# Reordering the last part of an output projection, and the first pair of the MLP behind it, in a decoder layer written as split float32 block products

## The chip, the cores and the metric

The kernel runs on one core of a Trainium2 chip. A core has five engines that run their own instruction streams side by side: TensorE (PE in the profile; its weight loads are PEld), VectorE (DVE), ScalarE (ACT), GpSimd (POOL) and SyncE (SP, which here only issues DMAs). Each stream runs in its written order, and semaphores tie the streams together. Matmul results land in PSUM; everything else lives in SBUF.

The metric is the device time of one launch in microseconds (us), the median of several runs. Lower is better.

## The reference

One decoder layer on x of shape 1 x 1024 positions x 1024 channels, all float32:

```python
h = rmsnorm(x, mix_norm[l])
proj = h @ w_in[l]
q, k, v, su, sv, g_a, g_b = jnp.split(proj, splits, axis=-1)
y_att = sliding_window_attention(q, k, v, q_norm[l], k_norm[l], sinks[l])
y_sgu = chunked_spatial_gating(su, sv, sgu_norm[l], w_s[l], b_s[l])
merged = (jax.nn.sigmoid(g_a) * (y_att @ w_oa[l])
          + jax.nn.sigmoid(g_b) * (y_sgu @ w_ob[l]))
x = x + merged @ w_out[l]
x = x + conv_gated_mlp(rmsnorm(x, ffn_norm[l]), w_up[l], conv_w[l], conv_b[l], w_down[l])
```

The change sits at `merged @ w_out` (the output projection, 1024 x 1024 x 1024), the squares for the second rmsnorm, and the first pair of column blocks of `@ w_up` (1024 x 5632).

## The kernel before

**Split float32.** A float32 operand is written as a high part (a float32r copy, made by ACT in `copy_hi`, L88) and a low part (the operand minus its high part, made by DVE for the moving side, by POOL for the weights). A product is three matmuls: high x high, high x low, low x high. So each operand costs one ACT copy and one subtraction before TensorE can use it.

**Seven products.** Large products are cut into 2 x 2 blocks and computed with seven block products in place of eight. The left side (weights) gives A11, A12, A22 and the sums S1 to S4; the right side (activations) gives B11, B21, B22 and the sums T1 to T4. The pairs are A11 B11, A12 B21, S1 T1, S2 T2, S3 T3, S4 B22 and A22 T4. Some products accumulate in PSUM onto a copy of another's result.

**The output projection** is 14 jobs, `out_job(0)` to `out_job(13)`. Job j works on product j // 2 of `O_STEPS` and on half e = j % 2 of the output rows: jobs 4 and 5 are S2 T2, 6 and 7 S1 T1, 8 and 9 S4 B22, 10 and 11 S3 T3, 12 and 13 A22 T4. A job is 24 matmuls (L1629) onto one of four PSUM tiles of 128 x 1024, X[0], X[1], Y[0], Y[1]. X[e] and Y[e] are reused: after jobs 4 and 5 an ACT copy (L1587) puts X[e] into Y[e], and S1 T1 accumulates on it.

`run_jobs` writes out the order. For job j it issues the matmuls, then the extra work that `O_WORK[j]` holds, then the split of the weights of job j + 2 (`o_split`: one ACT copy into `wjh`, two POOL subtractions into `wjl`, L1560), the load of the weights of job j + 4, and then the work on the result of job j, `o_post`. The `wjh` and `wjl` tiles are two deep, so the split for job j + 2 waits until TensorE has finished job j.

`o_post` forms a quarter of the new x (`final`, DVE, L1525), copies it out of PSUM (`keep`, ACT, L1520, and two stores), and makes the right-hand operands of the next product: `right_split`, `right_hi` and `right_lo` write the high and low parts of B11, T1, B22, T3, B21 (L88, L1503, L1510), `stt` (L1539) makes the sums B and Y. `square` takes a kept quarter to the square (ACT, L1531) and adds it to a running sum (POOL, L1533 and L1536). `o_late` holds a split that is run in the next job's `o_post`.

`m_hi`, `m_lo` (L1422) and `m_sum` (L664, L668) make the right-hand operands of the projection itself from `merged`.

**The first pair.** The MLP's up projection takes two column blocks (a pair) at a time: seven products of 12 matmuls each (L1112) onto `zg` (halves g0, g1) and `zv` (halves v0, v1). Each pair's left operands come from `Left`: `load_p`, `load_q`, `load_s3` load the raw blocks, `adds` makes S3 and S1 by two accumulating DMAs from POOL's queue (L1029, L1030), `sums_r` makes S2 and S4 on POOL (L664), and `split_p` (A11, A12), `split_q` (S1, A22), `split_s3` and `split_r` split them: ACT for the high part (L88), POOL for the low part (L1071). For pair 0 (`w0`) these are called from inside the projection. `first_pair` then issues pair 0; its `zv` and `zg` are the PSUM tiles that held Y[0] and Y[1]. Between its products stand the sum of squares over the channels (`ssq_cols`, 16 small matmuls, L1656), the power that makes the scale (POOL, L131), and, after the first product of pair 1, `rms_rows` (16 small matmuls, L140), which spreads the scale over the rows. From pair 1 on `fast_pair` repeats to pair 21.

Of the kernel before, what the change touches and what calls it, by code (L numbers as in the profile page):

```python
# [40 lines left out]
def body(ctx, tc, nc, a):  # L41
# [8 lines left out]
    def nm(s):  # L50
        uid[0] += 1
        return f"{s}_{uid[0]}"
# [1363 lines left out]
    def m_split(n, g):  # L1416
        m_hi(n, g)
        m_lo(n, g)
# [108 lines left out]
    def square(n, e):  # L1527

        q = pools["sq2"][:, (L, H)[int(n[1]) - 1]]
        t = pools["fp"].tile([128, 2, 512], F, tag="sqt", name=nm("sqt"))  # L1530
        nc.scalar.activation(t, ob[n][:, 2 * e:2 * e + 2, :], AF.Square)  # L1531
        if n in ("11", "12") and e == 0:
            nc.gpsimd.tensor_tensor(q, t[:, 0, :], t[:, 1, :], op=ALU.add)  # L1533
        else:
            for k in (0, 1):
                nc.gpsimd.tensor_tensor(q, q, t[:, k, :], op=ALU.add)  # L1536
# [18 lines left out]
    def o_split(r):  # L1555
# [8 lines left out]
        0: lambda: (m_hi("B21", 0), m_hi("B22", 0), out_load("11"), out_load("21")),  # L1564
        1: lambda: (m_split("T2", 0), m_split("T2", 1), m_lo("B22", 0), out_load("22")),
        2: lambda: (m_split("B22", 1), out_load("12")),
        3: lambda: (m_sum("T4", 0), m_sum("T4", 1), m_sum("T3", 0), m_sum("T3", 1)),
        4: lambda: (m_split("T4", 0), square("11", 0), w0.load_p(), w0.load_s3(), w0.load_q()),
        5: lambda: (m_split("T4", 1), square("11", 1), w0.adds()),
        6: lambda: (b11(0), m_split("T3", 0)),  # L1570
        7: lambda: (b11(1), m_split("T3", 1), w0.sums_r()),
        12: lambda: w0.split_s3(),
    }

    def b11(e):
        right_split("B11", e, ob["B"][:, 2 * e:2 * e + 2, :])

    def o_post(s, e):

        X, Yb = ob["X"][e], ob["Y"][e]  # L1580
        A, B = ob["A"], ob["B"]
        ds = (2 * e, 2 * e + 1)
        n = (None, "11", "21", "22", "12", "22", "21")[s]
        gs = [gain(n, d) for d in ds]
        ac = ob[n][:, 2 * e:2 * e + 2, :]
        if s == 2:
            nc.scalar.copy(Yb, X)  # L1587
        final(n, e, X if s in (2, 5, 6) else Yb, ac if s in (2, 3) else X if s == 6 else Yb,
              1.0 if s in (1, 4) else -1.0)
        for f in o_late:  # L1590
            f()
        o_late.clear()
        if s in (1, 4):
            for i, d in enumerate(ds):
                nc.scalar.activation((B if s == 1 else A)[:, d, :], Yb[:, i, :], AF.Copy, scale=gs[i][0])
            keep(n, e, Yb)
        if s in (5, 6):
            m, p = ("B22", Yb) if s == 5 else ("B21", X)
            for i, d in enumerate(ds):
                right_hi(m, d, p[:, i, :], gs[i][0])  # L1600
            keep(n, e, p)
            for i, d in enumerate(ds):
                right_lo(m, d, p[:, i, :], gs[i][0])
# [4 lines left out]
        if s == 5:  # L1608
            for i, d in enumerate(ds):
                stt(B[:, d, :], Yb[:, i, :], gs[i][1], B[:, d, :], ALU.subtract)  # L1610
            for i, d in enumerate(ds):
                stt(Yb[:, i, :], Yb[:, i, :], gs[i][1], A[:, d, :], ALU.add)
            o_late.append(lambda: right_split("T3", e, Yb))

    o_late = []
    SQ_AFTER = {9: ("12", 0), 10: ("12", 1), 12: ("22", 0), 13: ("22", 1)}

    def out_job(j):
        s, e = divmod(j, 2)
# [2 lines left out]
        def main(w):  # L1622
# [10 lines left out]
            yield  # L1633
            if j == 0:
                ob["Y"] = [PS("pY").rearrange("p (d c) -> p d c", d=2) for _ in range(2)]
            if s == 6:
                (w0.split_p, w0.split_q)[e]()
            if s == 0:
                nc.scalar.copy(ob["Y"][e], ob["X"][e])
            else:  # L1640
                o_post(s, e)
            if j in SQ_AFTER:
                square(*SQ_AFTER[j])
            if j == 13:
                psum["P"] = [psA, psA, psC_[0], psC_[0]]

# [89 lines left out]
    def first_pair():  # L1736
# [8 lines left out]
        fx = pools["fp"].tile([128, 4, 512], R, tag="hA", name="fax")  # L1745

        q.prod(q.v1, "A11", "B11")
        nc.scalar.copy(x1, q.v1)
        w.split(("S2", "S4"), w.r, *(fx[:, 2 * i:2 * i + 2, :].rearrange("p a (b m) -> p (a b) m", m=128)
                                     for i in (0, 1)))  # L1750
        nx.load_p()
        q.prod(q.g1, "S1", "T1")
        for e in (0, 1):
            right_split("T2", e, ob["B"][:, 2 * e:2 * e + 2, :])
        nc.scalar.copy(u2, q.g1)
        nx.load_q()
        nx.load_s3()
# [16 lines left out]
        nc.vector.tensor_tensor(q.g0, q.g0, x1, op=ALU.add)  # L1774
# [396 lines left out]
```

## Time and profile before

| | us |
|---|---|
| median of 3 runs (lowest to highest) | 1189.49 (1188.97 to 1190.51) |
| the profiled execution | 1190.27 |
| its span, first to last instruction | 1188.5 |
| TensorE busy in the span | 1164.3 (98%) |
| VectorE, GpSimd, ScalarE busy | 864.5, 664.4, 588.3 |
| mean granted TensorE clock | 0.993 |

The page gives the busy time of each engine, the span in 40 slices, the chain of work that ended last and the costliest groups. A busy TensorE there is not TensorE at its peak: matmuls are pipelined, and a matmul record of 0.39 us stands every 0.23 us. So the questions go to the timelines (each row: start, length, engine, line, operation, output <- inputs, and in brackets the idle time before it and what ended it) and to the table of waits (engine and tile that waited, who was waited for, total us, times, longest).

### The profile page before, as it was taken

How to read it: one execution, taken by the hardware profiler on the slowest of the kernel's cores; microseconds unless marked ns; L12 is line 12 of the kernel's file. 1: busy time of each engine (PE TensorE's matmuls, PEld its weight loads, DVE VectorE, ACT ScalarE, POOL GpSimd, SP SyncE). 2: the span in 40 equal slices, each digit the busy share in tenths (PEclk: the TensorE clock that was granted, in tenths of full speed). 3: DMA queues.
4: the chain of work that ended last, by engine and by line, in shares of the span. 5: the costliest groups of instructions: out<-in, count | busy, mean ns of one | idle time of the engine just before them, and what ended most of it. 6: DMA issues, size and time to landing. Idle time of an engine off the chain costs nothing.

```text
span 1188.5 us, 15815 instructions
## 1 busy us (share of the span) xinstructions
PE 1164.3 (98%) x5784; PEld 983.3 (83%) x5784; DVE 864.5 (73%) x985; ACT 588.3 (50%) x894; POOL 664.4 (56%) x460
## 2 busy tenths in 40 slices
PE   9999999999999999897999999999999999999998
PEld 9899999888888778685878888888888888888886
DVE  6787747635447889876788788877888797876674
ACT  6665668643436545565444444444344445425231
POOL 0668675589775756766967677776867641000000
PEclk9999999999999999998999999999999999999999
DMA  9343565275638665633645455455545258975561
GB/s 368 134 143 66 137 209 193 72 234 156 195 103 274 216 205 206 175 124 107 155 129 168 120 146 155 138 144 134 168 129 168 77 200 286 358 239 195 172 226 53
DMA packets 86429, 204.37 MB, mean 172 GB/s; under 512 B 9616, under 2 KB 17296, under 8 KB 86160
## 3 DMA queue, kind: packets, MB, share of 16 engines
q1 hardware_dynamic: 77280, 174.93, 42.7%
q0 software_dynamic: 8544, 19.93, 10.1%
q10 hardware_dynamic: 528, 8.52, 2.1%
q8 instruction: 45, 0.74, 0.2%
q14 instruction: 32, 0.26, 0.1%
HBM read 162.70 MB, written 57.41 MB: 185 GB/s over the span
## 4 chain that ended last, share of the span: by engine, by line
PE 79%; DVE 10%; POOL 4%; ACT 3%; issue 2%; DMA 2%; SPq 0%; DVEq 0%; POOLq 0%; ACTq 0%
PE pz L1112 46%; PE pdx L1983 8%; PE pd L1983 7%; PE pu L94 1%; PE pu L92 1%; PE pu L93 1%; PE pvs L92 1%; PE pvs L94 1%; PE pvs L93 1%; PE pv L560 1%; PE pq L92 1%; PE pq L94 1%; PE pq L93 1%; PE pY L1629 1%; DMA ra<-wdown 1%
## 5 line engine op out<-in xcount | busy, mean ns | idle before, releaser
L1112 PE MATMUL pz<-T,qh 128*128 128x512 f32 x472 | 148.2, 396 | 2.2 <-ACT qh L88 2.2
L1112 PE MATMUL pz<-B,ph 128*128 128x512 f32 x352 | 109.7, 393 | 0.3 <-ACT x L1817 0.2
L1112 PEld LDWEIGHTS pz<-T,qh 128*128 128x128 f32 x472 | 89.8, 191 | 21.6 <-ACT qh L88 2.6
L1071 POOL TENSOR_TENSOR pl<-lp,ph 128x1024 fp32r<-128x1024 f32 x30 | 74.4, 2481 | 49.7 <-ACT ph L88 49.7
L1112 PE MATMUL pz<-T,ql 128*128 128x512 f32 x236 | 93.5, 396 | 3.3 <-POOL ql L1071 3.3
L1112 PEld LDWEIGHTS pz<-B,ph 128*128 128x128 f32 x352 | 65.3, 188 | 16.3 <-ACT x L1817 3.2
L1130 DVE TENSOR_TENSOR pz<-pz,rstd_b 128x1024 f32<-128x1024 f32 x60 | 73.9, 1232 | 4.4 <-ACT rstd_b L143 2.4
L1071 POOL TENSOR_TENSOR ql<-lq,qh 128x1024 fp32r<-128x1024 f32 x30 | 76.7, 2555 | 0.0
L1112 PE MATMUL pz<-T,s3h 128*128 128x512 f32 x232 | 71.5, 389 | 0.0
L1112 PE MATMUL pz<-y,wjh 128*128 128x512 f32 x224 | 69.7, 392 | 0.9 <-ACT x L1366 0.6
L1983 PE MATMUL pdx<-bh,al 128*128 128x512 f32 x176 | 68.7, 390 | 0.2 <-DVE al L1954 0.2
L1983 PE MATMUL pdx<-bh,ah 128*128 128x512 f32 x176 | 68.6, 390 | 0.1
L1112 PE MATMUL pz<-B,pl 128*128 128x512 f32 x176 | 68.6, 390 | 0.0
L1983 PE MATMUL pdx<-bl,ah 128*128 128x512 f32 x176 | 68.5, 389 | 0.0
L1352 POOL TENSOR_TENSOR wjl<-wj,wjh 128x512 fp32r<-128x512 f32 (+1 forms) x32 | 41.9, 1332 | 33.6 <-ACT wjh L88 30.3
L1112 PE MATMUL pz<-T,AX 128*128 128x512 f32 x252 | 60.5, 389 | 0.0
L1112 PE MATMUL pz<-B,AX 128*128 128x512 f32 x252 | 60.5, 389 | 0.0
L1071 POOL TENSOR_TENSOR s3l<-lq,s3h 128x512 fp32r<-128x512 f32 x20 | 26.0, 1299 | 61.7 <-ACT s3h L88 61.7
L88 ACT ACTIVATE AX<-lr 128x1024 fp32r<-128x1024 f32 x21 | 22.3, 1063 | 70.3 <-POOL lr L664 70.3
L664 DVE TENSOR_TENSOR pz<-pz,u 128x512 f32<-128x512 f32 x37 | 25.9, 700 | 42.5 <-ACT u L1124 36.2
L1678 DVE SCALAR_TENSOR_TENSOR tg<-pz,cp,tg 128x1023 f32<-128x1023 f32 (+1 forms) x44 | 56.2, 1278 | 0.8
L1678 DVE SCALAR_TENSOR_TENSOR tv<-pz,cp,tv 128x1023 f32<-128x1023 f32 (+1 forms) x44 | 56.2, 1278 | 0.8
(380 smaller groups left out, 3607.6 us busy)
## 6 DMA issues: line engine op xcount, KB each, us to landing
lp<-wup SPq DMA_DIRECT2D x22, 512.0 KB, 3.8
lq<-wup SPq DMA_DIRECT2D x22, 512.0 KB, 4.1
ra<-wdown SPq DMA_DIRECT2D x44, 256.0 KB, 4.8
b<-T SPq DMA_DIRECT2D x44, 256.0 KB, 3.6
lq<-wup POOLq DMA_DIRECT2D x42, 256.0 KB, 5.2
B<-tv SPq DMA_DIRECT2D x33, 256.0 KB, 2.0
T<-tt SPq DMA_DIRECT2D x33, 256.0 KB, 2.2
b<-B SPq DMA_DIRECT2D x33, 256.0 KB, 3.0
```

The lines of the kernel that those rows point to most:

```text
L88: return nc.scalar.activation(dst, src, AF.Copy, scale=scale)
L92: nc.tensor.matmul(out, wh, mh, start=first, stop=False, **kw)
L93: nc.tensor.matmul(out, wh, ml, start=False, stop=False, **kw)
L94: nc.tensor.matmul(out, wl, mh, start=False, stop=last, **kw)
L560: nc.tensor.matmul(o, vhl[:, kb, g, :], w[:, 2 * g:2 * g + 2, :], start=i == 0 and g == 0, stop=i == len(ops) - 1, skip_group_check=True)
L664: eng.tensor_tensor(out, x, y, op=op)
L1071: nc.gpsimd.tensor_tensor(l, r, h.bitcast(F), op=ALU.subtract)
L1112: nc.tensor.matmul(o, p[:, k, :], m, start=not more and k == 0 and j == 0, stop=k == nk - 1 and j == 2, skip_group_check=True)
L1130: nc.vector.tensor_tensor(z, z, rstd_b, op=ALU.mult)
L1352: nc.gpsimd.tensor_tensor(l[:, k], r[:, k], h[:, k].bitcast(F), op=ALU.subtract)
L1678: nc.vector.scalar_tensor_tensor(t[:, j:], p[:, 0:1024 - j], cw[:, ci, 2 - j:3 - j], t[:, j:], op0=ALU.mult, op1=ALU.add)
L1983: nc.tensor.matmul(o[d], p[:, k - k0, m], q[:, k - k0, :], start=new and k == 0 and j == 0, stop=k == HK - 1 and j == 2, skip_group_check= ...
```

## The change

Nothing of the computation changes. What changes is where instructions stand in the streams:

- The split of `merged`'s T1 moves from the end of unit 6 of the branch stage to the middle of unit 7 (behind two ACT copies that TensorE needs).
- The sums for T3 and its splits move from jobs 3, 6 and 7 to jobs 5 to 8. The loads of pair 0's left operands move from job 4 to job 3.
- A second table, `O_AFTER`, holds work that is issued behind `o_post`: the squares, `adds`, and the two POOL sums of pair 0 (`sum_s2` in job 7, `sum_s4` in job 8) now stand behind the weights' split of the same job.
- The work after jobs 10 to 13 is written out in `post10` to `post13`.
- S1 of pair 0 is split alone after job 11, into the SBUF tile that held T3; A22 is split alone in `first_pair`.
- In `first_pair` the order of products was A11, S1, S3, A12, S2, S4, sum of squares, A22; it is now A11, S1, S3, S4, A12, S2, A22, sum of squares. T2's two high parts are now made ahead of its two low parts. The squares of quarter 21 are written over that quarter itself in place of the shared tile `sqt`, and the `adds` of pair 1 stand between their sums.

```diff
-        un["hooks"][6, 1] = lambda: (m_split("T1", 0), m_split("T1", 1))
+        un["hooks"][7, "x"] = lambda: (m_split("T1", 0), m_split("T1", 1))
...
-        t = pools["fp"].tile([128, 2, 512], F, tag="sqt", name=nm("sqt"))
+        if n == "21":
+            t = ob[n][:, 2 * e:2 * e + 2, :]
+        else:
+            t = pools["fp"].tile([128, 2, 512], F, tag="sqt", name=nm("sqt"))
...
-        3: lambda: (m_sum("T4", 0), m_sum("T4", 1), m_sum("T3", 0), m_sum("T3", 1)),
-        4: lambda: (m_split("T4", 0), square("11", 0), w0.load_p(), w0.load_s3(), w0.load_q()),
-        5: lambda: (m_split("T4", 1), square("11", 1), w0.adds()),
-        6: lambda: (b11(0), m_split("T3", 0)),
-        7: lambda: (b11(1), m_split("T3", 1), w0.sums_r()),
-        12: lambda: w0.split_s3(),
+        3: lambda: (m_sum("T4", 0), m_sum("T4", 1), w0.load_p(), w0.load_s3(), w0.load_q()),
+        4: lambda: m_split("T4", 0),
+        5: lambda: (m_split("T4", 1), m_sum("T3", 0)),
+        6: lambda: (b11(0), m_sum("T3", 1)),
+        7: lambda: (b11(1), m_split("T3", 0)),
+        8: lambda: m_split("T3", 1),
+    }
+    O_AFTER = {
+        4: lambda: square("11", 0),
+        5: lambda: w0.adds(),
+        7: lambda: (w0.sum_s2(), square("11", 1)),
+        8: lambda: w0.sum_s4(),
+        9: lambda: square("12", 0),
+        10: lambda: square("12", 1),
+        12: lambda: (w0.split_s3(), square("22", 1)),
...
+    def post10():
+        fin("22", 0)
+        o_late.pop()()
+        c_hi("22", "B22", 0, ob["Y"])
+        c_lo("22", "B22", 0, ob["Y"])
+        c22_sums(0)
+
+    def post11():
+        s1_split()
+        square("22", 0)
+        fin("22", 1)
+        right_split("T3", 0, ob["Y"][0])
+        c_hi("22", "B22", 1, ob["Y"])
+
+    def post12():
+        fin("21", 0)
+        c_lo("22", "B22", 1, ob["Y"])
+        c22_sums(1)
+        w0.split_p()
+        c_hi("21", "B21", 0, ob["X"])
+
+    def post13():
+        fin("21", 1)
+        right_split("T3", 1, ob["Y"][1])
+        c_lo("21", "B21", 0, ob["X"])
+        c_hi("21", "B21", 1, ob["X"])
+        c_lo("21", "B21", 1, ob["X"])
+
+    def s1_split():
+        t = Y(3, "s1", R, [128, 2, 4, 512])
+        w0.split(("S1",), w0.q[:, 0:4], *(t[:, 0, i].rearrange("p (k m) -> p k m", m=128) for i in (0, 1)))
...
-            if s == 6:
-                (w0.split_p, w0.split_q)[e]()
...
         q.prod(q.v1, "A11", "B11")
+        a22_split()
         nc.scalar.copy(x1, q.v1)
-        w.split(("S2", "S4"), w.r, ...)
+        fax_split()
         nx.load_p()
+        nx.load_q()
+        nx.load_s3()
         q.prod(q.g1, "S1", "T1")
...
         q.prod(q.v0, "S3", "T3")
+        square("21", 0)
+        nx.adds()
+        square("21", 1)
         nc.scalar.copy(x7, q.v0)
...
+        q.prod(q.g1, "S4", "B22", more=True)
+        q.prod(q.g0, "A12", "B21")
+        nc.vector.tensor_tensor(q.g0, q.g0, x1, op=ALU.add)
         sub(nc.vector, x7, x7, u2)
-        square("21", 0)
-        square("21", 1)
-        q.prod(q.g0, "A12", "B21")
-        nx.adds()
+        q.prod(q.v1, "S2", "T2", more=True)
         nx.split_p()
-        nc.vector.tensor_tensor(q.g0, q.g0, x1, op=ALU.add)
-        q.prod(q.v1, "S2", "T2", more=True)
-        q.prod(q.g1, "S4", "B22", more=True)
+        q.prod(q.v0, "A22", "T4", more=True)
         pb = q2.zv
         ratio = ssq_cols(pb)
...
-        q.prod(q.v0, "A22", "T4", more=True)
```

`c_hi` makes two high parts and the kept copy of a quarter, `c_lo` the two low parts, `c22_sums` the four sums B and Y, `fin` is `final`; they are the pieces of the old `o_post`, in another order. In the old one the kept copy stood between the high and the low parts in the same way, but everything of one job came in one block.

More of the change, by code (lines that the diff above doesn't have):

```diff
@@ L1596, in o_post @@
             keep(n, e, Yb)
[L1597 to L1603, printed above, removed]
         if s == 4:
@@ L1607, in o_post, with c_hi @@
             o_late.append(lambda: right_split("T1", e, B[:, 2 * e:2 * e + 2, :]))
[L1608 to L1613, printed above, removed]
+    def c_hi(n, m, e, p):
+        for i in (0, 1):
+            d = 2 * e + i
+            right_hi(m, d, p[e][:, i, :], gain(n, d)[0])
+        keep(n, e, p[e])
@@ new lines, in c_lo, with c22_sums, fin @@
+    def c_lo(n, m, e, p):
+        for i in (0, 1):
+            d = 2 * e + i
+            right_lo(m, d, p[e][:, i, :], gain(n, d)[0])
+    def c22_sums(e):
+        A, B, p = ob["A"], ob["B"], ob["Y"][e]
+        ds = (2 * e, 2 * e + 1)
+        for i, d in enumerate(ds):
+            stt(B[:, d, :], p[:, i, :], gain("22", d)[1], B[:, d, :], ALU.subtract)
+        for i, d in enumerate(ds):
+            stt(p[:, i, :], p[:, i, :], gain("22", d)[1], A[:, d, :], ALU.add)
+    def fin(n, e):
+        X, Yb = ob["X"][e], ob["Y"][e]
+        final(n, e, X, X if n == "21" else Yb, -1.0)
@@ new lines, in s1_split, with a22_split, fax_split @@
+    def s1_split():
+        t = Y(3, "s1", R, [128, 2, 4, 512])
+        w0.split(("S1",), w0.q[:, 0:4], *(t[:, 0, i].rearrange("p (k m) -> p k m", m=128) for i in (0, 1)))
+    def a22_split():
+        w0.split(("A22",), w0.q[:, 4:8], *(wst.tile([128, 8, 128], R, tag="w" + x, name=nm("q" + x))[:, 0:4] for x in "hl"))
+    def fax_split():
+        fx = pools["fp"].tile([128, 4, 512], R, tag="hA", name="fax")
+        w0.split(("S2", "S4"), w0.r, *(fx[:, 2 * i:2 * i + 2, :].rearrange("p a (b m) -> p (a b) m", m=128)
+                                       for i in (0, 1)))
@@ L1615, in body @@
     o_late = []
-    SQ_AFTER = {9: ("12", 0), 10: ("12", 1), 12: ("22", 0), 13: ("22", 1)}
     def out_job(j):
@@ L1640, in main @@
             else:
-                o_post(s, e)
-            if j in SQ_AFTER:
-                square(*SQ_AFTER[j])
+                {10: post10, 11: post11, 12: post12, 13: post13}.get(j, lambda: o_post(s, e))()
+            O_AFTER.get(j, lambda: None)()
             if j == 13:
```

9 lines of the change are left out of this document (3 added, 6 removed).

## The prediction

> **What bounds the kernel now.** The page gives TensorE 98% of the span, so only holes in its stream and slow stretches can be won. I read its waits first (who waited for whom: total us, times, longest), then its own timeline from job 4 of the projection to the first pair's end, then the busy times by stage (PE, PEld, DVE, ACT, POOL, each with its count; then the granted clock, the DMA share and GB/s).
>
> ```profile
> PE pz L1112 <- ACT x L1366: 0.6, 1, 0.6
> PE pY L1629 <- POOL wjl L1560: 0.6, 1, 0.6
> ...
> PE pd L1983 <- DVE bl L1954: 0.4, 1, 0.4
> ```
>
> ```profile
> 471.53 0.62 PE L1629 MATMUL pX<-mT,wjh 128*128 128x512 f32 x2
> ...
> 482.18 0.39 PE L1629 MATMUL pX<-mT,wjl 128*128 128x512 f32 x1
> 485.80 0.73 PE L1629 MATMUL pY<-mT,wjh 128*128 128x512 f32 x2 [3.23 <-ACT pY L1587]
> ...
> 501.84 0.70 PE L1629 MATMUL pY<-mB,wjh 128*128 128x512 f32 x2 [1.97 <-DVE ac L1525]
> ...
> 539.66 0.73 PE L1112 MATMUL pz<-T,qh 128*128 128x512 f32 x2 [2.21 <-ACT qh L88]
> 543.73 0.79 PE L1112 MATMUL pz<-T,ql 128*128 128x512 f32 x1 [3.34 <-POOL ql L1071]
> ...
> 553.67 2.88 PE L1112 MATMUL pz<-T,fax 128*128 128x512 f32 x12
> 558.20 3.01 PE L1112 MATMUL pz<-B,fax 128*128 128x512 f32 x12 [1.65 <-DVE pz L1774]
> 562.53 1.95 PE L1656 MATMUL pz<-ones,sq 128*128 128x2 f32 x16 [1.31 <-POOL sq L1536]
> 564.34 0.71 PE L1112 MATMUL pz<-T,qh 128*128 128x512 f32 x2
> ...
> 571.51 1.95 PE L140 MATMUL pz<-ident,ss8b 128*128 128x128 f32 x16
> 573.21 0.71 PE L1112 MATMUL pz<-B,ph 128*128 128x512 f32 x2
> ```
>
> ```profile
> 485.00:501.00 16.00, 13.40 (x48) 9.91 (x48) 14.56 (x6) 10.31 (x11) 15.84 (x13) 0.89 0.74 198
> 501.00:535.00 34.00, 33.16 (x146) 27.51 (x147) 26.09 (x28) 19.78 (x25) 24.90 (x16) 1.00 0.34 112
> 535.00:555.00 20.00, 14.45 (x53) 11.10 (x52) 14.72 (x15) 14.50 (x19) 10.73 (x6) 0.83 0.49 158
> 555.00:575.00 20.00, 17.03 (x83) 13.84 (x82) 7.67 (x8) 6.90 (x10) 17.77 (x13) 0.91 0.23 42
> ```
>
> Jobs 4 and 5 run without a wait from 471.53 to 482.41 (the last row's start plus the 0.23 between matmuls): 5.44 a job, 0.227 a matmul, 2.72 for the 12 of a product. Without waits, jobs 4 to 13 would end at 525.9, the seven products at 545.0, the 16 sums of squares (562.53 to 564.34) at 546.8, pair 1's first product at 549.5 and the 16 rows of the scale (571.51 to 573.21) at 551.2. They ended at 573.2: **22.0 lost**. The brackets and the 0.57 of the wait for wjl are 14.3 of it (3.23 + 0.57 + 1.97 + 2.21 + 3.34 + 1.65 + 1.31). The other 7.7 is mostly clock: the stages from 485, 535 and 555 hold 0.89, 0.83 and 0.91 of the clock where the one from 501 holds 1.00 (0.11 x 16 + 0.17 x 20 + 0.09 x 20 = 7.0). The wait for x (0.6, at 442.2) stands ahead of this and can go as well: 22.6 at most. Behind 573 no wait of TensorE is longer than the 0.4 for bl, so what is won there reaches the end.
>
> **The change part by part.** Each instruction stands at the later of its queue's last end and its inputs, on the clock on which TensorE never waits (job 8 starts at 493.3, 10 at 504.2, 12 at 515.1, 13 at 520.5; products at 525.9, 528.7, 531.4, 534.1, 536.8, 539.5, 542.3). Durations are those of before.
>
> *T1's split.* Its two ACT copies go behind the copy that job 14's third product waits for: **-0.6**. T1 is needed at 482; nothing else is late there.
>
> *Jobs 4 to 6.*
>
> ```profile
> 474.08 4.55 DVE L664 TENSOR_TENSOR mraw<-mraw,mraw 128x1024 f32<-128x1024 f32 x2
> 479.81 1.27 ACT L1595 ACTIVATE hB<-pY,cp 128x512 f32<-128x512 f32 x2 [5.86 <-DVE pY L1525]
> 484.72 1.03 ACT L1587 COPY pY<-pX 128x1024 f32<-128x1024 f32 x1
> ```
>
> ACT's queue waited 5.86 for `final`, which stood behind T3's two sums (4.55); so the copy into Y[0] (L1587) came at 484.7 to 485.75, 3.3 late. With the sums gone `final` starts at 474.1, and ACT goes on with hB (1.2), keep (0.9), T4 and wjh (0.95 each from start to start, 1.06 in the records) and the copy (1.03): done at 480.4, 2.0 early. The square moves behind it, off the path. POOL has wjl ready at 481, before its square. The 3.23, the 0.57 and this slow stretch go. The loads moved from job 4 to 3 stand ahead of job 7's weights in SP's queue; that split has over 2 us to spare.
>
> *Jobs 7 to 9.*
>
> ```profile
> 492.42 8.14 DVE L1422 TENSOR_TENSOR mT<-mraw,mT 128x1024 fp32r<-128x1024 f32 x1
> 492.54 5.68 POOL L1560 TENSOR_TENSOR wjl<-ow,wjh 128x512 fp32r<-128x512 f32 x4
> 500.48 1.21 DVE L1525 SCALAR_TENSOR_TENSOR ac<-pY,ac 128x1024 f32<-128x1024 f32 x1
> 502.75 2.31 DVE L1422 TENSOR_TENSOR mT<-mraw,mT 128x1024 fp32r<-128x1024 f32 x1
> ```
>
> Job 8 waited for a `final` that stood behind one T3 low part of 8.14 us (others 1.23): POOL ran four subtractions and a sum from 492.5 to 499.5, and DVE, whose two inputs lay in SBUF as POOL's did, got in only then (at 502.75 it waited for one instruction: 2.31). Now `final` of job 6 stands behind T3's second sum instead and is done at 491.8 (1.5 early); that of job 7 stands behind T3's first split, at 496.6 (2.2 early), if DVE takes its turn after one POOL instruction. The 1.97 goes.
>
> The Trainium skill, "SBUF — State Buffer", section "SBUF: two separate sides", says of the port pair that VectorE and GpSimd share that whichever starts first has it for the whole instruction and the other blocks. By that rule a two-input VectorE instruction waits 1.3 us at most; the 8.14 disagrees, and the measurement decides. It speaks against this change too, since GpSimd's queue now runs from 495 to 533 almost without a hole; its price is in the second rival.
>
> *S1 and the first pair.*
>
> ```profile
> 523.37 2.67 POOL L1536 TENSOR_TENSOR sq<-sq,sqt 128x512 f32<-128x512 f32 x2 [0.42 <-ACT sqt L1531]
> 530.63 1.30 POOL L1071 TENSOR_TENSOR s3l<-s,s3h 128x512 fp32r<-128x512 f32 x1 [2.08 <-ACT s3h L88]
> 531.89 2.40 POOL L1071 TENSOR_TENSOR pl<-lp,ph 128x1024 fp32r<-128x1024 f32 x1
> 538.54 1.06 ACT L88 ACTIVATE qh<-lq 128x1024 fp32r<-128x1024 f32 x1
> 511.04 1.41 DVE L1539 SCALAR_TENSOR_TENSOR hB<-pY,sink_b,hB 128x512 f32<-128x512 f32 x2 [2.24 <-ACT ac L1520]
> 566.76 1.67 POOL L131 TENSOR_TENSOR ss8b<-ss8b,mh 128x8 f32<-128x8 f32 x1
> DMA to landing us min/median/max: 2.0/2.9/4.7
> lq<-wup SPq DMA_DIRECT2D x5, 512.0 KB, 5.7
> ```
>
> The q split needed job 13's buffer and stood behind job 12's whole block: ACT at 538.5, POOL behind that and two squares; TensorE waited 2.21 + 3.34 and then ran slow. S1 alone (128 x 512: 0.65 on ACT, 1.3 on POOL, as s3l) follows job 11's end: ready near 521.8, wanted at 528.7. **What is late next** are three queues at once:
>
> - POOL has no hole from job 9's weights on (495.3: a pair of subtractions 2.5, a turn given to DVE 1.1, lr 1.25, squares 2.67; 502.9). Then subtractions for jobs 10 to 13 (four pairs of 2.5), lr 1.25, squares 1.3 + 2.67 + 2.67, S1 1.3, two turns given to DVE (1.1 each), then A11/A12's low part (2.4): 526.8, wanted at 526.4. TensorE waits **0.5**. Then s3l 1.3, squares 2.67, A22 1.3, S2/S4 2.4: 534.4, wanted at 535.0.
> - DVE from 521.3, where T3's first low part ends: `final` 1.14 (start to start), six operations of 0.7, `final` 1.14, 0.1 of waiting for ACT, T3's low part 1.23: 529.1. S1's result goes into Y[1], which that part still reads; wanted at 529.1.
> - ACT: A22, x1, S2/S4, T2 twice, then u2 at 534.3; S4, which writes on what u2 copies, is wanted at 534.6.
>
> The wait of 1.65 stood at S4, behind DVE's sum into g0 in the same PSUM tile; S2, in the other tile, had not waited for it. S4 is now issued ahead of that sum, so the wait goes. T4's parts (four sums of 0.7, two of 1.2) are ready near 542.2 and 543.4, wanted 0.8 later each. The squares of 21 are added by 543.8, the sum of squares starts at 545.5, so the 1.31 goes; the power (1.67) ends at 549.5 and the scale's rows start at 550.0. Before, the power ended 3.1 ahead of those rows; POOL's chain for pair 1 behind it (s3l, two sums, q: 6.2) now ends at 555.7, wanted at 557.6.
>
> *What I can't read:* how late pair 1's raw q lands, which `adds` now waits for between the squares of 21 (5.7 in the middle: 537.4, and POOL comes to `adds` at 539.3; the squares themselves wait for the stores of quarter 21, issued by 529.9 and at most 4.7 long: 534.6, when ACT comes to them at 535), whether the 16 small matmuls alone slow the clock (before, 1.31 of waiting stood ahead of them and the stage held 0.91), and DVE's turns at the port. Bounds: nothing for each, and twice the 5.7 for the load (543.1: 4 us on the squares' sum), 1.8 for the clock (0.09 of 20 us), 6.9 for one bad turn (8.14 - 1.23). I take nothing for the first two and one ordinary turn (1.1) plus 0.5 of small delays for the third, because seven inputs have less than 1 us to spare.
>
> **Sum:** -22.6 + 0.5 + 1.6 = -20.5 against the profiled 1190.27: 1169.8. The median of before stands 0.8 under that execution, so **1169.0**.
>
> **The rivals.**
>
> 1. *Forecast* (0.62): 1167 to 1171.5, small waits at A11, S1, S4 or A22.
> 2. *The port* (0.19): one two-input DVE instruction is kept out as at 492.42. In job 7 that is T3's first split with job 7's `final` behind it and job 9 behind that: 6.9 less 2.2 to spare, plus 1.8 of slow clock (0.11 of the 16 us behind job 6's wait): +6.5. In job 10 it is T1's low part, with `final` and job 13 behind it (1.1 to spare): +7.6. So 1174 to 1177. For it: POOL's queue has no holes. Against it: the 2.31 at 502.75, and `adds`, POOL's two DMAs ahead of the 8.14, now has a hole behind it.
> 3. *The load* (0.07): raw q takes twice its 5.7. POOL stands at `adds` until 543.1, 3.8 later than planned; the squares' sum, with 1.7 to spare, is 2.1 late, and pair 1's p, split behind it, 1 us more: 1172.
> 4. *The gain is handed back in pairs 1 and 2* (0.05): POOL's shorter lead, or the slow clock behind the small matmuls (1.8): 1170 to 1173.
> 5. *It doesn't do what it says* (0.03): the reused tiles (S1 where T3 lay, the squares over 21) or the order of PSUM tiles bring waits as long as those removed: 14.3 of waits and 7.7 of clock stay, 1189 give or take 2. Against it: in my queues none of these is over 1 us late.
> 6. *Slower* (0.04): the port again, as the rule in jobs 4 to 10, where ten two-input instructions of DVE stand (T4 and B11 twice, T3's sums and splits, T1 twice). Each costs 6.9; some 2 of each is hidden. It decides from the fifth on (5 x 4.9 = 24.5 against the 20.5): 1193, with a sixth 1198.
>
> **The numbers.** Cases 1 to 4 are faster (0.93), 5 the same, 6 slower; 0.2%, 2.4 us, is about what a measurement of this kernel can tell from no change. A range from 1166.4 (all 22.6 won, and 0.5 of spread between runs) to 1177 leaves out 5, 6 and the rare double of 2; it holds a little over 0.8.
>
> **What would show it.** T1: no wait for x at 442. Jobs 4 to 6: `final` follows T4's sums at once, and job 6 starts at job 5's end. Jobs 8, 9, 13: no wait for `final`, no DVE record above 2.5 us. First pair: no wait over 1 us at S1, S4 or the sums of squares; a wait of about 0.5 for pl at A11. The granted clock is 1.00 from 440 to 600. The prediction is wrong if TensorE still waits over 3 us anywhere there, most likely for DVE behind POOL in jobs 7 to 13, or if new waits stand in pairs 1 to 3.

## The result, and the profile after

The changed kernel takes **1168.38 us** (median of 4 runs, 1167.89 to 1169.80) against 1190.0 (4 runs beside them, 1188.97 to 1191.21): a ratio of 0.982, 95% interval 0.9803 to 0.9837. The forecast was 1169.0. The profiled execution has a span of 1168.0 against 1188.5, so 20.5 less.

TensorE's table of waits after (who waited for whom: total us, times, longest), its longest lines:

```profile
PE pz L1112 <- ACT x L1878: 3.3, 1, 3.3
PE rb L140 <- DVE qs L345: 1.1, 1, 1.1
PE warm L255 <- POOL rstd_b L120: 1.1, 1, 1.1
...
PE pY L1692 <- ACT pY L1700: 0.3, 1, 0.3
```

Every wait that the prediction quoted between jobs 6 and the scale is gone, the 0.6 for x (L1366) too, and a new one leads: 3.3 for x at L1878. The matmul line of the projection is L1692 now, the others shift by up to 61 lines. The stages of the projection and of the first pair, in the table of busy times (PE, PEld, DVE, ACT, POOL; then granted clock, DMA share, GB/s):

```profile
485.00:501.00 16.00, 16.00 (x72) 13.28 (x71) 12.54 (x10) 9.62 (x11) 15.03 (x11) 1.00 0.52 132
501.00:535.00 34.00, 34.00 (x151) 28.05 (x151) 29.41 (x31) 30.05 (x38) 31.88 (x23) 1.00 0.52 166
535.00:555.00 20.00, 20.00 (x106) 17.05 (x105) 14.66 (x17) 9.90 (x12) 17.75 (x13) 1.00 0.36 99
...
573.00:580.00 7.00, 5.12 (x12) 4.05 (x13) 6.88 (x7) 3.88 (x5) 3.49 (x4) 0.58 0.19 65
```

TensorE is busy for all of each of the first three stages, at a clock of 1.00, where before it had 0.89 and 0.83 in two of them; GpSimd has 31.88 of the 34.00 us in the second. Behind them stands a stage at 0.58. TensorE's timeline shows both:

```profile
480.65 0.62 PE L1692 MATMUL pY<-mT,wjh 128*128 128x512 f32 x2
...
523.94 0.39 PE L1692 MATMUL pX<-mT,wjl 128*128 128x512 f32 x1
...
526.94 2.90 PE L1112 MATMUL pz<-T,s 128*128 128x512 f32 x12
...
532.41 2.89 PE L1112 MATMUL pz<-B,fax 128*128 128x512 f32 x12
...
574.88 1.22 PE L1112 MATMUL pz<-B,ph 128*128 128x512 f32 x2 [3.28 <-ACT x L1878]
```

Jobs 6 to 13 run from 480.65 to 524.17 (the start of the second row and the 0.23 between matmuls) without a bracket, S1 (`s`) follows A11 at 526.94, S4 (`fax`) follows S3 at 532.41. Then, in pair 2, A12 waits 3.28 us for x1's copy.

**Where the time came from.** I set the start of the same matmul of both traces side by side. Job 0 starts at 449.21 before and at 447.30 after (1.91 earlier); the matmul after the scale's rows at 573.21 and 549.56 (23.65 earlier); pair 2's S2 at 603.80 and 586.03 (17.77); the last matmul of all 20.51 earlier. So 1.9 came before the projection, **21.7** in the projection and first pair, **5.9 went back** in pair 2, and 2.7 came after it.

### The profile page after: what moved, and what is told of

Same layout as the page of the kernel before. It is cut to its first block, busy times and chain, and to the rows that moved or that the text cites. A ratio compares the mean times of both kernels' runs of the same rounds, so it can differ in the third digit from the quotient of the medians.

```text
span 1168.0 us, 15816 instructions
## 1 busy us (share of the span) xinstructions
PE 1156.0 (99%) x5784; PEld 981.8 (84%) x5784; DVE 853.7 (73%) x985; ACT 589.7 (50%) x895; POOL 661.0 (57%) x461
## 4 chain that ended last, share of the span: by engine, by line
PE 90%; DVE 3%; POOL 3%; ACT 1%; DMA 1%; issue 1%; SPq 0%; DVEq 0%; POOLq 0%; ACTq 0%
PE pz L1112 51%; PE pdx L2044 10%; PE pd L2044 8%; PE pY L1692 2%; PE pX L1692 2%; PE pvs L94 1%; PE pvs L93 1%; PE pvs L92 1%; PE pu L94 1%; PE pu L92 1%; PE pu L93 1%; PE pv L560 1%; PE pq L92 1%; PE pq L94 1%; PE pq L93 1%
## 5 line engine op out<-in xcount | busy, mean ns | idle before, releaser
L1112 PE MATMUL pz<-T,qh 128*128 128x512 f32 x464 | 143.3, 390 | 0.0
L1112 PEld LDWEIGHTS pz<-T,qh 128*128 128x128 f32 x464 | 87.3, 188 | 18.5 <-ACT u L936 0.3
L1112 PE MATMUL pz<-T,ql 128*128 128x512 f32 x232 | 90.3, 389 | 0.0
L1071 POOL TENSOR_TENSOR ql<-lq,qh 128x1024 fp32r<-128x1024 f32 (+1 forms) x30 | 75.7, 2522 | 0.1
L88 ACT ACTIVATE qh<-lq 128x1024 fp32r<-128x1024 f32 (+1 forms) x30 | 31.4, 1047 | 69.6 <-POOL pl L1071 28.1
L1112 PEld LDWEIGHTS pz<-B,AX 128*128 128x128 f32 x252 | 47.3, 188 | 9.8
```

Source lines behind the costliest of these rows:

```text
L88: return nc.scalar.activation(dst, src, AF.Copy, scale=scale)
L1071: nc.gpsimd.tensor_tensor(l, r, h.bitcast(F), op=ALU.subtract)
L1112: nc.tensor.matmul(o, p[:, k, :], m, start=not more and k == 0 and j == 0, stop=k == nk - 1 and j == 2, skip_group_check=True)
```

## The experiments

Twelve kernels, each the changed kernel with one edit. Besides the medians I give d1, the time from job 0's first matmul to the matmul behind the scale's rows, and d2, from there to the last matmul, both against the changed kernel (102.27 and 613.30 us in its trace), because the start of a run varies by more than some of these effects: in the changed kernel and the eleven of these that have its instructions ahead of 440, job 0 starts between 446.22 and 449.44. Each d1 and d2 comes from one trace; in the four kernels whose edit lies outside of it (u_t1 and the three m_) d1 agrees within 0.2.

| kernel | median us | d1 | d2 |
|---|---|---|---|
| before | 1190.0 | +21.7 | -3.1 |
| changed | 1168.4 | 0 | 0 |
| u_t1 (one run) | 1170.1 | -0.2 | -0.4 |
| u_t3 | 1170.9 | +4.2 | -1.4 |
| u_sq | 1174.8 | +6.7 | -0.7 |
| u_s1 | 1171.9 | +2.3 | -2.2 |
| u_order | 1172.9 | +5.3 | -3.7 |
| u_loads | 1169.2 | -0.1 | +0.5 |
| u_squares | 1169.8 | +1.9 | -2.0 |
| u_sums (one run) | 1170.2 | +1.6 | -2.0 |
| u_sqloads | 1172.0 | +3.8 | -1.5 |
| m_adds | 1165.4 | -0.1 | -4.2 |
| m_x1 | 1169.5 | -0.1 | -0.4 |
| m_both | 1165.4 | -0.1 | -4.8 |

### The parts, one undone at a time

**T1's split** back at its old place:

```diff
-        un["hooks"][7, "x"] = lambda: (m_split("T1", 0), m_split("T1", 1))
+        un["hooks"][6, 1] = lambda: (m_split("T1", 0), m_split("T1", 1))
```

> The changed kernel with T1's two splits at their old place, ahead of the copy of x in job 14 of the stage before. Theory: TensorE waits 0.6 for x again, seen near 440 in its waits; nothing else moves. Rival: the wait was chance, none is seen.

TensorE waited 0.59 us at 441.23 for x L1366, as before. From the matmul at 438 to that at 445 it lost 0.88 against the changed kernel, the kernel before 0.92: the wait and 0.3 that no bracket shows. So that part is worth 0.9, a little more than its 0.6; it stands ahead of d1.

**T3's sums** back in job 3:

```diff
-        3: lambda: (m_sum("T4", 0), m_sum("T4", 1), w0.load_p(), ...
-        5: lambda: (m_split("T4", 1), m_sum("T3", 0)),
-        6: lambda: (b11(0), m_sum("T3", 1)),
+        3: lambda: (m_sum("T4", 0), m_sum("T4", 1), m_sum("T3", 0), m_sum("T3", 1), w0.load_p(), ...
+        5: lambda: m_split("T4", 1),
+        6: lambda: b11(0),
```

> The changed kernel with T3's two sums (4.55 us together on VectorE in the kernel before) back behind T4's in job 3. Theory (they hold up job 4's scaled sum, ScalarE's hB and the copy that job 6 waits for): job 6 waits 2.0 to 2.6 us for that copy, with up to 1.75 of slow clock: 1170 to 1173. Rival (the square that stood ahead of the copy on ScalarE was the larger part, and it is gone): a wait under 0.6: 1168 to 1169.

The timeline of DVE, ACT and PE in that kernel, and its stage behind the wait:

```profile
471.25 4.56 DVE L664 TENSOR_TENSOR mraw<-mraw,mraw 128x1024 f32<-128x1024 f32 x2
...
476.99 1.27 ACT L1607 ACTIVATE hB<-pY,cp 128x512 f32<-128x512 f32 x2 [5.86 <-DVE pY L1525]
...
482.03 0.73 PE L1692 MATMUL pY<-mT,wjh 128*128 128x512 f32 x2 [2.32 <-ACT pY L1599]
```

```profile
482.00:485.50 3.50, 3.47 (x10) 2.65 (x11) 2.79 (x2) 3.50 (x4) 3.50 (x4) 0.68 0.22 73
```

The same 5.86 us of ScalarE waiting as before is back, the two sums ahead of it, and 2.32 of the former 3.23 at job 6; the 0.9 between them is about the square (1.06 on ScalarE), which stayed behind. With the slow stretch that follows the part is worth 4.2. The theory held.

**S1 split with A22** again, into buffers that job 13 must free:

```diff
-        s1_split()            # job 11
-        a22_split()           # behind A11 of the first pair
+        w0.split_q()          # job 13, ahead of its other work
```

> The changed kernel with S1 and A22 split together again (1.06 on ScalarE, 2.4 on GpSimd), into the buffers of the projection's weights, behind job 13's matmuls. Theory (the shared split needs job 13's buffer, so it can start at 524 only, behind a pair of squares on GpSimd to 527.0): ql is ready at 529.4, S1's third matmul wants it at 527.4, so a wait of about 2 us stands at S1, with up to 1.75 of slow clock: 1170 to 1173. Rival (the 2.21 and 3.34 of the kernel before came from the squares ahead of it on GpSimd, which are behind it now): a wait under 0.7, 1168 to 1169.

TensorE waited 0.38 for VectorE at S1's first matmul and 1.47 for `ql` at its third: d1 +2.3. The theory's place and size held. It was 5.55 before (2.21 + 3.34). Two squares stood ahead of `ql` on GpSimd both times; but before, ScalarE's copy `qh` came 4.0 us behind the end of job 13 (538.54 and 534.57), here with it (525.14 and 525.17). So about a third of that wait, 1.85, belongs to the shared split, the rest to what stood ahead of ScalarE's copy and of the squares.

**The old order of products**, A11, S1, S3, A12, S2, S4, the sums of squares, A22:

```diff
-        q.prod(q.g1, "S4", "B22", more=True)
         q.prod(q.g0, "A12", "B21")
...
         q.prod(q.v1, "S2", "T2", more=True)
         nx.split_p()
-        q.prod(q.v0, "A22", "T4", more=True)
+        q.prod(q.g1, "S4", "B22", more=True)
         pb = q2.zv
         ratio = ssq_cols(pb)
...
         lefts[2].load_p()
+        q.prod(q.v0, "A22", "T4", more=True)
```

> The changed kernel with the order of products of the kernel before in the first pair: A11, S1, S3, A12, S2, S4, the sums of squares, A22; all other queues as changed. Theory (S4 waits for VectorE's sum in the same PSUM tile): that sum is at 540.74 to 541.43, S4 is wanted at 537.86, so a wait of 3.5 us stands at S4 with a slow stretch behind it (1.7 to 2.6), and the power comes no earlier, so pair 2's wait stays: 1172 to 1175. Rival (the order was worth only the 1.65 of the kernel before, and the earlier sum of squares gives GpSimd its lead back in pair 2): 1164 to 1170.

```profile
540.80 4.62 PE L1112 MATMUL pz<-B,fax 128*128 128x512 f32 x12 [3.42 <-DVE pz L1833]
```

S4 waited 3.42 for VectorE's sum, and its 12 matmuls took 4.62 where they took 2.89: +5.3. The second half of the expectation was wrong: with the sums of squares ahead of A22 the power does come earlier against TensorE, and pair 2's wait fell from 3.3 to 0.5 (d2 -3.7). That points at GpSimd's lead, which the next kernels test.

### Pair 2's new wait

The chain behind the 3.28, in GpSimd's and ScalarE's timelines of the changed kernel:

```profile
545.63 2.05 POOL L131 TENSOR_TENSOR ss8b<-ss8b,mh 128x8 f32<-128x8 f32 x1 [2.09 <-DVE ss8b L130]
...
553.82 0.93 POOL L1029 DMA_DIRECT2D lq<-wup  x1
554.46 1.19 POOL L1030 DMA_DIRECT2D lq<-wup  x1
...
560.40 1.30 POOL L1071 TENSOR_TENSOR s3l<-lq,s3h 128x512 fp32r<-128x512 f32 x1 [2.33 <-ACT s3h L88]
```

```profile
559.69 0.63 ACT L88 ACTIVATE s3h<-lq 128x512 fp32r<-128x512 f32 x1 [3.78 <-DMA lq<-wup]
...
568.85 1.06 ACT L88 ACTIVATE AX<-lr 128x1024 fp32r<-128x1024 f32 x1 [5.68 <-POOL lr L664]
569.82 0.57 ACT L1124 COPY u<-pz 128x512 f32<-128x512 f32 x1
573.15 1.20 ACT L1733 ACTIVATE tv<-pz,cp 128x1024 f32<-128x1024 f32 x1 [2.76 <-DVE pz L1130]
574.25 0.58 ACT L1878 COPY x<-pz 128x512 f32<-128x512 f32 x1
```

Read upward: x1's copy stands behind the first tap of pair 1's convolution (L1733), which waited 2.76 for VectorE; VectorE had waited 2.15 for u's copy, and that stands behind AX (the high part of S2 and S4), which waited 5.68 for GpSimd's `lr` (their raw sums); GpSimd had waited for `s3h`, and ScalarE for the accumulating loads, which GpSimd issued only after the power and pair 1's four operations. GpSimd stood idle 2.09 us ahead of that power.

**The loads into the hole** (m_adds):

```diff
         nx.split_p()
+        lefts[2].adds()
         q.prod(q.v0, "A22", "T4", more=True)
...
         nx.split_q()
-        lefts[2].adds()
         lefts[2].load_p()
```

> The changed kernel with one edit: pair 2's two accumulating loads (0.93 + 1.19 us on GpSimd at 553.82) are issued ahead of the sum of squares, in the hole that GpSimd has there (543.54 to 545.63), not behind pair 1's q. Theory A (GpSimd's chain, anchored on the power behind the sum of squares, makes ScalarE's copy AX late, and x1 stands behind it): AX comes 2 to 3.5 us earlier, x1 is ready at its wanted 571.4, TensorE's wait of 3.28 in pair 2 falls below 1 us and the slow stretch behind it (2.6 us lost) goes: 1162 to 1164. Rival B (VectorE's chain from the 2.93 us difference at 564.74 sets x1): at most 1.5 of the 3.28 goes, 1166 to 1168. Rival C (the slow stretch comes from the small matmuls of the sum of squares, not from the wait): the wait goes, the clock in pair 2 stays slow, 1165.

Its ScalarE and TensorE timelines, and the stage that held 0.58:

```profile
557.90 0.63 ACT L88 ACTIVATE s3h<-lq 128x512 fp32r<-128x512 f32 x1
...
567.11 1.06 ACT L88 ACTIVATE AX<-lr 128x1024 fp32r<-128x1024 f32 x1 [3.37 <-POOL lr L664]
...
573.53 0.61 PE L1112 MATMUL pz<-B,ph 128*128 128x512 f32 x2
```

```profile
573.00:580.00 7.00, 7.00 (x33) 5.79 (x32) 5.77 (x6) 3.95 (x6) 3.01 (x3) 1.00 0.31 44
```

No wait for the load, AX 1.7 us earlier in a trace whose TensorE was 2.1 later at the scale, no wait at A12 (573.53), a clock of 1.00. Theory A held, rival C fell; rival B had no room, since the difference (1.09 at 564.83 there, 2.93 in the changed kernel) sped up with GpSimd's row. 1165.4 (1164.84 to 1167.69; ratio to before 0.9801, 0.9786 to 0.9815) is below all four runs of the changed kernel, though the intervals of the two ratios overlap (0.9803 to 0.9837 there). It is also a little more than the 1162 to 1164 expected, for a reason that d2 shows: at pair 2's S2 it had won 6.4 us against the changed kernel since the scale, at the end 4.2.

**x1's copy ahead of the tap** (m_x1):

```diff
             prev.last_sum()
-            prev.tap_v()
+            n == 2 or prev.tap_v()
...
         nc.scalar.copy(x1, q.g0)
+        if n == 2:
+            prev.tap_v()
```

> The changed kernel with one edit: in pair 2 ScalarE copies x1 ahead of pair 1's first tap (1.0 us, which waits 2.76 for VectorE), not behind it. GpSimd's chain and AX stay as late as they were. Theory A (x1 is late only because it stands in ScalarE's queue behind AX, u's copy and the tap): x1 goes at 570.5 to 571.2, right behind u's copy, the wait of 3.28 goes and the slow stretch with it: 1162 to 1164. Rival B (what is late is the data behind it, pair 1's last sums): the tap is late and with it the taps on VectorE and the next writer of that PSUM tile; a new wait of 1 to 3 us stands at pair 3's first product: 1166 to 1169.

The 3.28 went, but AX was as late as ever, and TensorE waited 0.57 for pair 2's x7, 1.28 for VectorE at its S4, and 1.47 for x1 in pair 3. Nothing was won: the queue position was the symptom and GpSimd's lateness the cause. Theory A fell here, and the rival named too few places.

**Both, x1 first in every pair** (m_both), beside the edit of m_adds:

```diff
             prev.last_sum()
-            prev.tap_v()
...
         nc.scalar.copy(x1, q.g0)
+        if not rms:
+            prev.tap_v()
```

> The kernel with the early accumulating loads (1165.4 us), and in every pair from the second on ScalarE copies x1 ahead of the pair before's first tap, not behind it. In that kernel the wait of 3.28 in pair 2 was gone and the clock full, and yet TensorE lost 2.2 us again between pair 3 and the end, by gaps of 0.05 to 0.11 us at the first matmul behind x1's copy, one in each two pairs, and some 1.2 at the start of the down projection. Theory (x1's copy, behind the tap that waits 2.76 for VectorE, is what is late by that little): those gaps (0.8 together) go, with others of 0.005 that follow them, 1164 to 1165. Rival (pair by pair TensorE is paced by VectorE's own chain): the gaps only move, to x7's or to S2's first matmul, 1165 to 1166.

From pair 2 on the small gaps were gone, as the theory said: by the clock of the traces this kernel stays 4.78 ahead of the changed one from pair 2's S2 to the down projection, where the lead of m_adds falls from 4.33 to 3.25. But the down projection then waited 0.58 and 0.27 for VectorE, and the median is that of m_adds: 1165.36 (ratio 0.9793, 0.9777 to 0.9809). All runs of both lie below all runs of the changed kernel; between the two there is no measured difference.

This explains part of d2. TensorE in the changed kernel, held up in pair 2, meets hardly a gap from there to the end. The kernels that came through pair 2 faster by 2.6 us or more (u_sq, u_order, u_squares, u_sums, u_sqloads, m_adds) lose 1.9 to 2.5 of it again behind; u_t3 and u_s1, faster by 1.4 and 2.3, lose nothing. So a TensorE that runs behind the other engines meets no gaps, and one that runs closer to them does. That is also the 2.7 which the kernel before lost behind pair 2. And since pair 2 itself costs less in most of these kernels (its wait of 3.28 is 2.28 in u_s1 and 0.48 in u_order), undoing a part costs less at the end (d1 + d2) than where it stands.

### The port in jobs 6 to 9

**Squares, loads and sums of pair 0** back ahead of the weights (u_sq):

```diff
-        4: lambda: m_split("T4", 0),
-        5: lambda: (m_split("T4", 1), m_sum("T3", 0)),
+        4: lambda: (m_split("T4", 0), square("11", 0)),
+        5: lambda: (m_split("T4", 1), m_sum("T3", 0), square("11", 1), w0.adds()),
...
-        7: lambda: (b11(1), m_split("T3", 0)),
+        7: lambda: (b11(1), m_split("T3", 0), w0.sums_r()),
```

> The changed kernel with the squares of quarter 11, pair 0's accumulating loads and its two sums for S2 and S4 back ahead of the weights' splits in jobs 4, 5 and 7, as in the kernel before; all the rest as changed. Theory of the port (what kept VectorE out for 8.14 us was the four subtractions and two sums that GpSimd ran one behind the other straight after the accumulating loads): a low part of T3 of over 5 us comes back in jobs 6 to 9, job 8 or 9 waits 2 to 6 us for VectorE, up to 1.75 of slow clock: 1171 to 1176. Rival, queues alone (GpSimd's own lateness: 1.3 to 2.7 a square, 2.1 for the loads, 2.5 for the sums): no record of VectorE above 3 us, waits for a weight's low part of 0.3 to 1.5 in jobs 6 to 8: 1168.5 to 1170.

```profile
486.44 0.92 POOL L1029 DMA_DIRECT2D s<-wup  x1
...
487.06 1.21 POOL L1030 DMA_DIRECT2D lq<-wup  x1
...
487.53 8.10 DVE L664 TENSOR_TENSOR mraw<-mraw,mraw 128x1024 f32<-128x1024 f32 x1
...
487.63 5.66 POOL L1563 TENSOR_TENSOR wjl<-ow,wjh 128x512 fp32r<-128x512 f32 x4
...
492.65 1.88 POOL L664 TENSOR_TENSOR lr<-lq,lp 128x512 f32<-128x512 f32 x1
...
494.62 2.15 POOL L664 TENSOR_TENSOR lr<-lp,lr 128x512 f32<-128x512 f32 x1
```

The 8.14 us is back as 8.10, of another instruction (a sum of T3 in place of its low part), against the same row of GpSimd: four subtractions and two sums. VectorE was out for five of the six. The second sum reads the first one's result and starts 0.08 behind its end; there VectorE got in, and that sum took 2.15 where one alone takes 1.25 to 1.3. TensorE waited 2.54 for a weight and 1.99 for VectorE, and d1 is +6.7. Theory of the port: held. Then one ingredient at a time, the same lines of u_sq's edit singly: the loads alone (u_loads), the squares alone (u_squares), the sums alone (u_sums). The cuts leave out the lines of `O_AFTER` from which each is taken.

```diff
# u_loads
+        5: lambda: (m_split("T4", 1), m_sum("T3", 0), w0.adds()),
# u_squares
+        4: lambda: (m_split("T4", 0), square("11", 0)),
+        5: lambda: (m_split("T4", 1), m_sum("T3", 0), square("11", 1)),
# u_sums
+        7: lambda: (b11(1), m_split("T3", 0), w0.sums_r()),
```

> The changed kernel with one of the three parts that the kernel of all three (1174.8 us, where VectorE was kept out for 8.10 us again) put back: only pair 0's accumulating loads stand ahead of job 7's weights on GpSimd. They take 2.1 us and so let the subtractions of two jobs pile up. Theory 1 (VectorE is kept out when GpSimd runs several ready subtractions straight behind its accumulating loads): a two-input record of VectorE of 5 us or more comes back near 487 to 492, with a wait of 1 to 3 us at job 8: 1170 to 1173. Theory 2 (it takes the squares' lateness as well, so that four subtractions and two sums stand ready): no record of VectorE above 3 us, no wait above 0.6: 1168 to 1169.

> The changed kernel with only the squares of quarter 11 back ahead of the weights' splits in jobs 4 and 5; the accumulating loads stay behind job 7's weights. Theory 1 (the loads ahead of ready subtractions are what keeps VectorE out): no record of VectorE above 3 us, waits only for a weight's low part that GpSimd gives late, 0.3 to 2.5 us in jobs 6 to 8: 1168.5 to 1172. Theory 2 (any pile of ready GpSimd work does it): VectorE has a record of 4 us or more in jobs 6 to 8.

> The changed kernel with only pair 0's two sums for S2 and S4 (1.25 to 1.3 us each on GpSimd) back to back ahead of job 9's weights. Theory 1 (the loads matter, not the sums): no record of VectorE above 3 us and no new wait above 0.5 in jobs 7 to 9: within 1 us of the changed kernel. Theory 2 (a row of ready GpSimd work is enough): VectorE's second low part of T3, 1.84 us at 494.63, takes 4 us or more.

The loads alone did nothing (no record above 2.31, d1 -0.1): theory 1 in that form fell. The other two fit neither theory. The sums cost a wait of 1.29 for a weight where under 0.5 was expected; and the record of 3.29 in that kernel, between the theories' 3 and 4, stands ahead of the moved sums, in a row that it shares with the changed kernel, so the edit is not shown to have made it. The squares gave a record of 4.41, above theory 2's 4, but not against just any pile of GpSimd's work. VectorE's timeline in u_squares, then GpSimd's:

```profile
487.39 2.29 DVE L664 TENSOR_TENSOR mraw<-mraw,mraw 128x1024 f32<-128x1024 f32 x1
...
491.87 4.41 DVE L1422 TENSOR_TENSOR mT<-mraw,mT 128x1024 fp32r<-128x1024 f32 x1
```

```profile
486.32 4.51 POOL L1563 TENSOR_TENSOR wjl<-ow,wjh 128x512 fp32r<-128x512 f32 x2
490.78 0.93 POOL L1029 DMA_DIRECT2D s<-wup  x1
491.39 1.22 POOL L1030 DMA_DIRECT2D lq<-wup  x1
491.97 3.21 POOL L1563 TENSOR_TENSOR wjl<-ow,wjh 128x512 fp32r<-128x512 f32 x2
```

Against the pair of subtractions at 486.32 VectorE waits for one (2.29 = 1.2 of its own and 1.1), and the pair takes 4.51, since GpSimd then waits in turn. Against the same pair directly behind the accumulating loads VectorE waits for both: 4.41 = 3.2 + 1.2, and the pair takes 3.21. In u_sums it was 3.29 against two, in u_t3 3.47; in u_loads the subtractions waited 0.17 for ScalarE behind the loads, and nothing happened. So the new theory: directly behind its loads GpSimd keeps the port for as long as it has instructions ready. The last kernel (u_sqloads), squares and loads but not the sums, has four ready:

```diff
+        4: lambda: (m_split("T4", 0), square("11", 0)),
+        5: lambda: (m_split("T4", 1), m_sum("T3", 0), square("11", 1), w0.adds()),
```

> The changed kernel with the squares of quarter 11 and pair 0's accumulating loads back ahead of the weights' splits, and the two sums for S2 and S4 left behind. Each of the three parts alone gave no record of VectorE above 4.41 us; behind the loads with two subtractions ready VectorE was out for both (4.41 and 3.29), behind the loads with a hole of 0.17 it was not. Theory 1 (VectorE stays out as long as GpSimd has ready instructions in a row directly behind its accumulating loads): with four subtractions ready the record near 487 takes 5.5 to 7 us, 1.1 to 2.6 less than the 8.10 with the two sums; job 8 waits for a low part and job 9 for VectorE less than the 1.99 of that kernel: 1170 to 1174. Theory 2 (the sums, which read the tile that the loads write, are needed for it): no record above 4.5 us, only the lateness of GpSimd: 1169 to 1172.

```profile
486.91 1.22 POOL L1030 DMA_DIRECT2D lq<-wup  x1
...
487.39 6.86 DVE L664 TENSOR_TENSOR mraw<-mraw,mraw 128x1024 f32<-128x1024 f32 x1
...
487.49 5.67 POOL L1563 TENSOR_TENSOR wjl<-ow,wjh 128x512 fp32r<-128x512 f32 x4
```

6.86 is the 5.67 of the four and VectorE's own 1.2, and 1.24 less than the 8.10, the length of one sum; TensorE waited 2.52 and 0.75, d1 +3.8. As a price the theory held. As a rule it has a gap, in the changed kernel itself:

```profile
486.80 1.19 POOL L1030 DMA_DIRECT2D lq<-wup  x1
...
487.26 1.21 DVE L664 TENSOR_TENSOR mraw<-mraw,mraw 128x1024 f32<-128x1024 f32 x1
...
487.38 4.51 POOL L1563 TENSOR_TENSOR wjl<-ow,wjh 128x512 fp32r<-128x512 f32 x2
```

Here VectorE's sum starts 0.12 us ahead of two ready subtractions behind the loads and goes first; in the kernel before the low part started about as far ahead (492.42 and 492.54) and was out for five. The six kernels that keep these rows of the changed one (u_t1, u_s1, u_order and the three m_) all have it as there. But u_sums has the same instructions up to here too. There the pair ahead of the loads started 0.8 us earlier (35.53 us behind job 0's start, in the changed kernel 36.35), and VectorE lost to the pair behind the loads with B11's low part (the 3.29). So what is shown is that a VectorE instruction which loses there is out for the whole ready row. Which of two that start so close together goes first stays open, and so does why the loads matter.

## Why the prediction came out right, and where it was wrong

*The bound and the 22.0 to be won.* Right: job 0 to the scale's rows gave 21.7, and undoing the parts brought their waits back where the prediction had put them. Undone singly they come to 18.5 (4.2 + 6.7 + 2.3 + 5.3); the other 3.2 no single undoing shows. The split of the 22.0 is a little off, not its sum: of the 7.0 given to the clock, 1.2 fell into a wait (a clock of 0.65 over the 3.34 us up to 543.73 before), and a wait cost more than its bracket in u_t1 (0.88 for 0.59).

*T1.* Right in its place, 0.9 against 0.6. The other 1.0 ahead of job 0 is none of the change's: it is there at 300 us already.

*Jobs 4 to 6.* Right: `final` behind T3's sums, with ScalarE's 5.86, was the mechanism.

*Jobs 7 to 9.* Right that the wait for `final` goes with the 8.14. Rival 2, the port, did not come: no single record of VectorE there is above 2.3. The reason given against it, a hole behind the loads, was wrong: two subtractions stand ready there, and VectorE went first by a margin that before was not enough. So the prediction does not explain that it did not come, and in u_sums the same row fell the other way. What the change does lower is the price: two in place of five are ready, so a loss there would cost 2 to 3 us (3.29 to 4.41 less 1.2) in place of 6.9.

*S1 and the first pair.* Right in all its places. The 0.5 for `pl` did not come (`pl` ended at 524.4, wanted at 524.6), nor the 1.6 allowed for the port and small delays. The unread items are answered: `adds` issued at once, and the small matmuls alone did not slow the clock (1.00 from 535 to 555).

*POOL's lead: the step that failed.* The prediction followed GpSimd's chain to pair 1's q and stopped there (done at 553.9, in time as forecast). Behind it stood the accumulating loads for pair 2, five more operations on GpSimd and AX, in front of x1's copy. This was rival 4, with 1170 to 1173 and a chance of 0.05; it happened, and it cost 5.9 (3.28 and a slow stretch), which rival 4's span of 1 to 4 us did not hold. By the prediction's own signs this part is wrong: it named a new wait in pairs 1 to 3 as one, and a clock of 1.00 up to 600, where 573 to 580 had 0.58.

So **the number is right because errors cancel**: to the 22.6 less 2.1 of allowance the runs answer with 21.7 and 0.9, less 5.9, plus 2.7 of later gaps that vanished because TensorE had been held up, plus 1.0 of chance. That it came within 1 us is luck. With the wait mended 1165.4 was there, below the forecast's range of 1166.4 to 1177.

## What to carry to other kernels

When an anchor moves (here the power, which came 21 us earlier, at 545.63 in place of 566.76, but ended 0.2 ahead of TensorE's rows of the scale in place of 3.1), follow each engine's queue behind it until it waits for TensorE again, not only to the next deadline: the loads that it issues late are the next stage's wait. Issue DMAs in a hole ahead of the anchor rather than behind it. And measure a part where it stands as well as at the end: a later wait that shrinks in turn, or the gaps that a held-up engine no longer meets, can hide a third of it or more (T3's 4.2 left 2.8 at the end, S1's 2.3 almost nothing).

## What the runs showed of the hardware

**How long the port is lost depends on what GpSimd did just before.** The Trainium skill, "SBUF — State Buffer", section "SBUF: two separate sides", says that whichever engine starts first holds the shared pair for the whole instruction. In ordinary rows the traces agree (VectorE 2.3 in place of 1.2, then GpSimd late in turn). Directly behind GpSimd's accumulating loads they do not: where VectorE lost, it was out for more than one instruction. In jobs 6 to 9 it was out until the end of two (3.29, 3.47, 4.41), four (6.86) and five (8.10, 8.14), in four of these six cases although its own record starts 0.1 us ahead of theirs; in the other two it came during the first. The same stands behind the loads for pair 3 in the changed kernel: a difference of half the size took 2.93 at 564.74, in m_adds 1.09, and its record ends behind GpSimd's subtraction and first sum. Within the rows of jobs 6 to 9 in which VectorE lost, each GpSimd record starts 0.7 us before the end of the one ahead of it (0.56 to 0.64 ahead of a sum; in u_squares 491.97 to 493.93, then 493.22); where VectorE got its turn it starts 0.04 before it (in the changed kernel 487.38 to 489.64, then 489.60). Whether that is why VectorE stays out, no run shows.

**The length of a wait alone doesn't decide on a slow stretch.** u_t3's wait of 2.32 at job 6 was followed by a clock of 0.68 over the 3.5 us from 482. In u_sqloads, TensorE waited 2.52 at job 7, and the clock held:

```profile
486.00:489.50 3.50, 0.98 (x6) 0.48 (x4) 3.50 (x3) 2.95 (x3) 3.50 (x5) 1.00 0.44 63
489.50:493.00 3.50, 3.50 (x15) 2.91 (x16) 3.50 (x1) 0.00 (x0) 3.50 (x3) 1.00 0.80 139
```

After pair 2's 3.28 in the changed kernel the clock was at 0.58 over 7 us; in u_sq pair 2 waited longer, 3.48 at 582.15, and the clock was 1.00 over the 10 us from 580. The Trainium skill, "TensorE: Matmul & The Clock Gate", section "Part 1: The HAM clock gate", tells of an activity window of about 3.4 us that runs freely, and of the slow state after an idle one. That the same wait can fall well or badly agrees with a free window; that 2.32 us, less than a window, are enough does not agree with an idle one, and the measurement decides.
